# Attention heads sent in pairs, and the values of the sink heads held stationary

## The chip, the cores and the metric

The kernel runs on one core of a Trainium2 chip. The metric is the device time of one execution in microseconds (us): the median of three runs is 1763.69 us, the lowest 1762.58 and the highest 1768.16. Below, TensorE is the matrix engine (PE in the rows, its weight loads PEld), VectorE is DVE, ScalarE is ACT, and SP is the engine that issues the loads.

## The reference, cut to what matters

Two model blocks follow each other; everything is float32, 256 tokens of width 1024. The first block (three recurrent branches and a feed-forward) is not touched. The second block runs two layers over the stream `x` and, in the first layer only, over 256 tokens of context `ctx`. In each layer the normed tokens are projected, and the mixing has three parts whose outputs, 256 + 512 + 256 columns wide, go through `w_out`:

```
a  gated MLP over chunks of 128 tokens
b  8 query heads of 64, 2 key heads: softmax(q k^T / 8 with a sink logit) v
     p = softmax([window scores, context scores, sink]);  o = p_window v + p_ctx v_ctx
c  4 differential heads: softmax(q1 k1^T) - lam softmax(q2 k2^T), times v, then a norm
```

Queries of `x` see 512 keys (256 of the stream, of which a window mask leaves |q - k| <= 128, and 256 of the context). Queries of the context see the 256 context keys. The sink is one more logit per head: it enters the sum of the softmax, and has no value.

## The kernel before

Products are done in float32 precision by splitting each operand into a high and a low part and summing three products (high x high, high x low, low x high); this holds for all projections (`gemm_ws`, `gemm_xs`, `mm3`) and for the scores. Every weight comes from memory as a tile of up to 512 KB (`weight_raw`), is cast to its high part by ScalarE (L383) and its low part is taken by VectorE (L385). The products of the probabilities with the values are plain float32, which the trace shows as two instructions each.

`layer` (from L1364) handles one layer of the second block. Queries, keys and values of 128 tokens are a tile; `t` 0 and 1 are the stream, 2 and 3 the context. `unit` projects, `qk_part` norms and rotates queries and keys and transposes them into `qkh` and `qkl` (heads on partitions: two heads of 64, or four maps of 32, per column of blocks). `HEADORDER` puts heads j and j + 4, which belong to different key heads, side by side, so that a pair lies on rows 0 to 63 and 64 to 127.

`attention` (from L1609) sends a list of items through a pipeline of steps, a `yield` after each. A query tile has 12 items: 8 window heads and 4 differential heads. In a step, `scores` is emitted for an item two ahead, `transposed` for one, `values` for the one before, and `finished` for one still older:

- `scores` calls `probs` once for a window head and twice for a differential head. `probs` takes a bank of the pool `c`, sends three products (L1517 to L1519, 64 or 32 rows, 128 columns stationary, 512 or 256 streaming) and for the tiles 0 and 1 of a window head adds the mask as a product with an identity over 256 columns (L1521). VectorE takes the maximum (L1523) and makes the bias from it (L1525, L1527); ScalarE takes the exponential and its sum (L1529).
- `transposed` turns the probabilities over in blocks of 128 on TensorE (L1562) into one bank of the pool `s`; ScalarE copies them to SBUF (L1564).
- `values` multiplies: the transposed probabilities are stationary, the 128 columns of the values stream (L1574). For a window head the product holds both key heads, and half of it is used. After four heads VectorE divides by the sum with the sink, straight from the bank of the pool `o` into `OB` (L1585).
- `finished` transposes `OB` (L1606) and splits it into `XH` and `XL`, from which `out_proj` multiplies by `w_out`.

Tiles 3 and 2 of layer 0 run between the projections of the stream, four steps after each unit; tiles 1 and 0 of layer 0 run with the output projection of the context, a weight after the steps in `Knobs.fill`; in layer 1 only tiles 1 and 0 run, with steps of the modulation after the steps in `Knobs.afill`. PSUM has eight banks, shared out by `psum`: two for projections (`g`), three for scores (`c`), one for outputs (`o`) and two for transposes (`s`); in the attention of layer 1, four for scores, one for outputs, two for transposes and one for the modulation (`a`).

The program is written in the order above, but each engine's final order is made by the framework's scheduler when it is built: in the trace, pieces of neighbouring steps and projections stand between each other. Within the built program every engine works in its given order; TensorE's records, though, show products on different rows starting side by side.

Of the kernel before, what the change touches and what calls it, by code (L numbers as in the profile page):

```python
# [10 lines left out]
F32 = mybir.dt.float32  # L11
# [17 lines left out]
# columns of the modulations done on the tensor engine, 512 at a time, and on the vector engine, 128  # L29
# [4 lines left out]
# column offsets of the first block's w_in  # L34
# [4 lines left out]
# rows of the small projections: i gates, f gates, dt  # L39
# [3 lines left out]
def _ws(name, layer, c0, nk=8, r0=0):  # L43
    """[nk*128, 128] block of a weight, rows on partitions, 128 columns."""
    def cut(w):
        return w[name][layer][r0:r0 + nk * 128, c0:c0 + 128].reshape(nk, 128, 128).transpose(1, 0, 2)
# [12 lines left out]
def _ada(layer, c0, q):  # L59
    """[256, 512] block: rows on partitions, 512 columns."""  # L60
# [27 lines left out]
def _qcols(c):  # L88
    """256 columns of the window attention's queries, heads j and j + 4 side by side."""
    return np.concatenate([np.arange(512 + 64 * h, 576 + 64 * h) for h in HEADORDER[4 * c:4 * c + 4]])  # L90

# [33 lines left out]
def plan2(layer):  # L125
# [10 lines left out]
    p += [(("out", j), _ws("w_out_2", layer, 128 * j)) for j in range(8)]  # L136
# [12 lines left out]
def _cols(v):  # L149
    """[n*128] -> [128, n]"""  # L150
# [3 lines left out]
def _convc(w):  # L154
    """[K, n*128] -> [128, n*K]"""
# [121 lines left out]
class Knobs:  # L277
# [11 lines left out]
    fill = (2, 6, 10, 14, 18, 22, 24, 26)  # L289
    afill = tuple(range(20, 30))  # L290
# [9 lines left out]
def tile_two_blocks(ctx: ExitStack, tc: tile.TileContext, xT, ctxT, cst1, cst, cstw, pb1, pl0, pl1, pf0, pf1, pc, pcb, wb, w0, w1, out,  # L300
# [16 lines left out]
    class PS:  # L317
        """PSUM pools of the phase at hand"""

    def psum(**bufs):  # L320
        """Shares out the eight banks: name=number."""
# [3 lines left out]
        for nm in "asgcpo":  # L325
            if nm not in bufs:
                setattr(PS, nm, None)

# [64 lines left out]
    def gained(dst_h, dst_l, x, g):  # L393
        """x g, split: what the first products after a norm take; 1 / rms is applied to their results"""
# [4 lines left out]
    def mm3(o, w, rhs, nk, late=False, first=True, last=True):  # L399
        """o = W^T x in three passes; late: the low part of x comes last."""  # L400
# [19 lines left out]
    def gemm_xs(ph, keys, lhs, toks, evac):  # L420
        """out[128 tokens, 256 features]; lhs(k, t) gives (high, low) of a token tile."""
        w = [weight(ph, k, 256) for k in keys]
        for t in toks:
            ps = PS.g.tile([128, 512], F32, tag="g", name="psx")
# [11 lines left out]
    def rsqrt_raw(pool, a, n, tag, bufs, rows=128):  # L436
        """RS * result = 1 / sqrt(a)"""
# [3 lines left out]
        # in two halves, so that neither waits for the step before  # L441
# [13 lines left out]
    def mean_sq(x, scale=None, eps=EPS):  # L455
        """mean of squares + eps, [128 tokens, 2 blocks of them], in PSUM"""
# [20 lines left out]
    def rms_all(a):  # L477
        """[128, 256] on every partition: 1 / (RS sqrt(a)) for tokens on partitions"""
# [44 lines left out]
    def ada_pe(li):  # L523
        """512 columns at a time on the tensor engine; both parts of the conditions share a pass."""
# [35 lines left out]
    def ada_rows(pool):  # L560
        """twice silu(c) of both conditions, on every partition"""
# [9 lines left out]
    def ada_dve(li):  # L571
        """128 columns at a time, on partitions: products summed along the rows"""
# [11 lines left out]
    def ada_tick():  # L584
        """After each weight tile: now and then a step."""
# [16 lines left out]
    # =====================================================================  # L602
    # convolution, SwiGLU, down projection
    # =====================================================================
    def ffn(ph, pool, halves, xh, xl, cw3, cb, causal, resid, hook=None, mid=None, raw=None):
        """halves: 1 or 2 blocks of 256 tokens. With two, the first columns take the second block first and the
        last rows the first block first, so that neither waits for the other's norms."""
# [20 lines left out]
        def down(j0, j1, m, rhs, n):  # L628
            ps = PS.g.tile([128, 512], F32, tag="g", name="psg")
# [7 lines left out]
        for j0, j1 in CHUNKS:  # L637
            hid = []
            for j in range(j0, j1):
# [3 lines left out]
                elif j == 0:  # L643
                    # as many as there are buffers take the second block first
                    w = [weight(ph, ("up", e // 2, e % 2), 128) for e in range(3)]
                    first = [PS.g.tile([128, 512], F32, tag="g", name="psg") for _ in range(3)]
# [36 lines left out]
    # =====================================================================  # L683
    # first block
# [1084 lines left out]
```

## Time and profile before

| What | Value |
|---|---|
| median of 3 runs | 1763.69 us |
| lowest, highest | 1762.58, 1768.16 us |
| profiled execution, first to last instruction | 1767.7 us |
| TensorE busy | 1738.8 us, 98% |
| VectorE busy | 1384.8 us, 78% |
| ScalarE busy | 983.7 us, 56% |
| mean granted TensorE clock | 0.991 of full |
| the 16 DMA engines, main queue | 49.8% of their span |

The profile is of one execution, and its own time is known as its span, 1767.7 us, which lies among the three runs, near the highest. Busy times of TensorE include the modelled end of each product, so products that stream behind each other overlap in it: the start of one row to the start of the next is what a product keeps the engine for. A timeline row merges equal instructions that follow each other: start, length, engine, line, operation, output and inputs, shape (rows*columns of the stationary part, then what streams), count, and in brackets the idle time before it.

### The profile page before, as it was taken

How to read it: one execution, taken by the hardware profiler on the slowest of the kernel's cores; microseconds unless marked ns; L12 is line 12 of the kernel's file. 1: busy time of each engine (PE TensorE's matmuls, PEld its weight loads, DVE VectorE, ACT ScalarE, POOL GpSimd, SP SyncE). 2: the span in 40 equal slices, each digit the busy share in tenths (PEclk: the TensorE clock that was granted, in tenths of full speed). 3: DMA queues.
4: the chain of work that ended last, by engine and by line, in shares of the span. 5: the costliest groups of instructions: out<-in, count | busy, mean ns of one | idle time of the engine just before them, and what ended most of it. 6: DMA issues, size and time to landing. Idle time of an engine off the chain costs nothing.

```text
span 1767.7 us, 31912 instructions
## 1 busy us (share of the span) xinstructions
PE 1738.8 (98%) x12442; PEld 1568.2 (89%) x12442; DVE 1384.8 (78%) x2716; ACT 983.7 (56%) x1723; POOL 0.2 (0%) x4
## 2 busy tenths in 40 slices
PE   7999999999999999999999999999999999999999
PEld 7999988878888999999878898888888997799999
DVE  7987967557778996877687799999656878788776
ACT  6655645445556865666676564442244556766554
POOL 0000000000000000000000000000000000000000
PEclk8999999999999999999989999999999999999999
DMA  7555445447677666654211356657433543046564
GB/s 233 159 154 152 138 132 157 147 126 222 218 228 228 187 190 221 209 170 139 86 67 47 105 163 189 183 171 232 129 96 107 168 132 120 24 141 195 174 196 132
DMA packets 80502, 276.97 MB, mean 157 GB/s; under 512 B 9056, under 2 KB 13792, under 8 KB 80224
## 3 DMA queue, kind: packets, MB, share of 16 engines
q1 hardware_dynamic: 80352, 274.94, 49.8%
q8 instruction: 98, 1.61, 0.4%
q14 instruction: 52, 0.43, 0.1%
HBM read 273.86 MB, written 1.05 MB: 156 GB/s over the span
## 4 chain that ended last, share of the span: by engine, by line
PE 51%; DVE 3%; ACT 1%; issue 0%; ACTq 0%
PE psg L404 12%; PE psg L407 12%; PE psg L406 11%; PE pso L1574 3%; PE psx L429 2%; PE psx L431 2%; PE psx L430 2%; PE psp L1562 2%; PE psc L1517 1%; PE psc L1519 1%; PE psc L1518 1%; DVE wl L385 0%; ACT Pp L1529 0%; DVE mx L1523 0%; PE psc L1521 0%
## 5 line engine op out<-in xcount | busy, mean ns | idle before, releaser
L383 ACT CAST wh<-raw 128x1024 fp32r<-128x1024 f32 (+1 forms) x475 | 490.9, 1037 | 531.0 <-PE psg L406 423.7
L385 DVE TENSOR_TENSOR wl<-raw,wh 128x1024 fp32r<-128x1024 f32 (+1 forms) x475 | 572.5, 1208 | 206.8 <-ACT wh L383 203.2
L404 PE MATMUL psg<-XH,wh 128*128 128x256 f32 (+1 forms) x1288 | 400.7, 314 | 3.6 <-ACT XH L390 1.9
L407 PE MATMUL psg<-XH,wl 128*128 128x256 f32 (+1 forms) x1288 | 398.8, 312 | 0.3 <-DVE wl L385 0.3
L406 PE MATMUL psg<-XL,wh 128*128 128x256 f32 (+1 forms) x1240 | 387.5, 313 | 0.7 <-DVE XL L1304 0.5
L404 PEld LDWEIGHTS psg<-XH,wh 128*128 128x128 f32 x1288 | 243.0, 189 | 22.0 <-ACT XH L390 2.3
L407 PEld LDWEIGHTS psg<-XH,wl 128*128 128x128 f32 x1288 | 243.3, 189 | 15.9 <-DVE wl L385 1.0
L406 PEld LDWEIGHTS psg<-XL,wh 128*128 128x128 f32 x1240 | 234.5, 189 | 16.1 <-DVE XL L1304 1.1
L404 PE MATMUL psg<-xh,wh 128*128 128x256 f32 x704 | 203.4, 289 | 1.8 <-ACT xh L390 1.3
L406 PE MATMUL psg<-xl,wh 128*128 128x256 f32 x704 | 200.5, 285 | 0.9 <-DVE xl L391 0.9
L407 PE MATMUL psg<-xh,wl 128*128 128x256 f32 x704 | 200.1, 284 | 0.3 <-DVE wl L385 0.3
L404 PE MATMUL psg<-hh,wh 128*128 128x256 f32 (+1 forms) x592 | 179.6, 305 | 0.1
L407 PE MATMUL psg<-hh,wl 128*128 128x256 f32 (+1 forms) x592 | 178.5, 302 | 0.0
L406 PE MATMUL psg<-hl,wh 128*128 128x256 f32 (+1 forms) x592 | 178.5, 302 | 0.0
L404 PEld LDWEIGHTS psg<-xh,wh 128*128 128x128 f32 x704 | 134.9, 192 | 6.0 <-ACT xh L390 1.5
L406 PEld LDWEIGHTS psg<-xl,wh 128*128 128x128 f32 x704 | 135.1, 192 | 2.9 <-DVE xl L391 1.4
L407 PEld LDWEIGHTS psg<-xh,wl 128*128 128x128 f32 x704 | 134.9, 192 | 2.2 <-issue 1.3
L406 PEld LDWEIGHTS psg<-hl,wh 128*128 128x128 f32 x592 | 111.5, 188 | 5.3 <-DVE hl L391 0.2
L404 PEld LDWEIGHTS psg<-hh,wh 128*128 128x128 f32 x592 | 110.9, 188 | 5.9 <-ACT hh L390 0.6
L407 PEld LDWEIGHTS psg<-hh,wl 128*128 128x128 f32 x592 | 111.2, 188 | 5.5
L429 PE MATMUL psx<-wh,XH 128*128 128x256 f32 x384 | 110.0, 287 | 1.1 <-DVE ss L1379 0.5
L430 PE MATMUL psx<-wh,XL 128*128 128x256 f32 x384 | 108.5, 283 | 0.0
(435 smaller groups left out, 3237.8 us busy)
## 6 DMA issues: line engine op xcount, KB each, us to landing
raw<-w SPq DMA_DIRECT2D x254, 512.0 KB, 3.7
raw<-wb SPq DMA_DIRECT2D x197, 512.0 KB, 4.3
araw<-w SPq DMA_DIRECT2D x40, 512.0 KB, 4.2
raw<-w SPq DMA_DIRECT2D x16, 384.0 KB, 3.4
raw<-wb SPq DMA_DIRECT2D x8, 384.0 KB, 3.2
xres<-xT SPq DMA_DIRECT2D x16, 128.0 KB, 3.6
plt<-pl SPq DMA_DIRECT2D x2, 588.0 KB, 5.5
xres<-ctxT SPq DMA_DIRECT2D x8, 128.0 KB, 2.7
```

The lines of the kernel that those rows point to most:

```text
L383: S.copy(wh[:, 0:sz], raw[:, 0:sz])
L385: V.tensor_tensor(wl[:, 0:sz], raw[:, 0:sz], wh[:, 0:sz], ALU.subtract)
L404: T.matmul(o, wh[:, k], xh, start=(first and k == 0), stop=False)
L406: T.matmul(o, wh[:, k], xl, start=False, stop=False)
L407: T.matmul(o, wl[:, k], xh, start=False, stop=(last and not late and k == nk - 1))
L429: T.matmul(o, xh, wh[:, k % 4], start=(k == 0), stop=False)
L430: T.matmul(o, xl, wh[:, k % 4], start=False, stop=False)
L431: T.matmul(o, xh, wl[:, k % 4], start=False, stop=(k == 7))
L1517: T.matmul(o, qh, kh, start=True, stop=False)
L1518: T.matmul(o, qh, kl, start=False, stop=False)
L1562: T.transpose(ps[:, b], p[:, b * 128:(b + 1) * 128], ident)
L1574: T.matmul(po[:, i % 4], pt[:, b], v, start=(b == 0), stop=(b == nb - 1))
```

## The change

The items of a query tile become 8: four pairs of window heads and four differential heads. `scores` sends the two tiles of an item alternately: high x high of both, then high x low of both, then low x high of both. The mask is a product over the 128 columns in which there is anything masked, once for each tile of a pair. `transposed` takes up to four blocks per bank: a pair with 512 keys fills two banks, the first copied by ScalarE, the second by VectorE. For window heads, `values` holds 64 columns of the values stationary and streams the transposed probabilities, so that the output comes with features on partitions, the two heads of a pair in the halves. The division by the sum is therefore along the free dimension: the reciprocal is broadcast over 64 partitions by a product with the identity into a bank of `s`, copied by ScalarE, and multiplied in by VectorE; the result is split into `XH` and `XL` without a transpose. `OB` and `finished` are for the differential heads alone. The order of the features changes with it, and so do the rows of `w_out` (`_mixrows`, done when the weights are laid out).

The banks of the first and second stage become `c` 4, `o` 1, `s` 3, and projections take theirs from `s` (`PS.gtag`); in the attention of layer 1 the shares stay. `fill` and `afill` follow the shorter list of steps. All other differences are comments. Its core:

```diff
-    fill = (2, 6, 10, 14, 18, 22, 24, 26)
-    afill = tuple(range(20, 30))
+    fill = (1, 3, 6, 8, 11, 13, 15, 17)
+    afill = tuple(range(10, 20))
...
+        PS.gtag = "g"
+        if PS.g is None:
+            PS.g, PS.gtag = PS.s, "s"
...
-        ps = PS.g.tile([128, 512], F32, tag="g", name="psg")
+        ps = PS.g.tile([128, 512], F32, tag=PS.gtag, name="psg")
...
-        psum(g=2, c=3, o=1, s=2)
+        psum(c=4, o=1, s=3)
...
         def scores(A, i):
...
+            rows = []
+            for e in range(2):
+                if i < 4:
+                    d = slice(64 * e, 64 * e + 64)
+                    rows.append((d, i, 4, 2 * i + e, L.nsink[:, 2 * i + e:2 * i + e + 1]))
+                else:
+                    m = 2 * i - 8 + e
+                    d = slice(32 * (m % 4), 32 * (m % 4) + 32)
+                    rows.append((d, 5 + m // 4, 7 + m // 4, 10 + m, None))
+            ps = [PS.c.tile([128, 512], F32, tag="c", name="psc") for _ in range(2)]
+            kk = slice(A.k0, A.k0 + A.nk)
+            mask = i < 4 and A.t < 2
+            for q_, k_, n in ((qkh, qkh, 0), (qkh, qkl, 1), (qkl, qkh, 2)):
+                for e, (d, jq, jk, h, _) in enumerate(rows):
+                    T.matmul(ps[e][:, 0:A.nk], q_[d, jq, A.tq], k_[d, jk, kk], start=(n == 0),
+                             stop=(n == 2 and not mask))
+            if mask:
+                o = slice(128 * (1 - A.t), 128 * (1 - A.t) + 128)
+                for e in range(2):
+                    T.matmul(ps[e][:, o], identb, winb[:, A.t, o], start=False, stop=True)
...
+        def transposed(A, pp):
+            out = []
+            blocks = [(p, b) for p in pp for b in range(A.nb)]
+            for i in range(0, len(blocks), 4):
+                some = blocks[i:i + 4]
+                ps = PS.s.tile([128, 4, 128], F32, tag="s", name="psp")
+                for n, (p, b) in enumerate(some):
+                    T.transpose(ps[:, n], p[:, b * 128:(b + 1) * 128], ident)
+                pt = ap.tile([128, 4, 128], F32, tag="PT", name="PT", bufs=Knobs.ptb)
+                if i:
+                    V.tensor_copy(pt[:, 0:len(some)], ps[:, 0:len(some)])
+                else:
+                    S.copy(pt[:, 0:len(some)], ps[:, 0:len(some)])
+                out += [pt[:, n] for n in range(len(some))]
+            return [out[j:j + A.nb] for j in range(0, len(out), A.nb)]
...
         def values(A, i, pt):
...
+            if i < 4:
+                for b in range(nb):
+                    for e in range(2):
+                        d = slice(64 * e, 64 * e + 64)
+                        T.matmul(po[d, i], BV[:, kb0 + b, d], pt[e][b], start=(b == 0), stop=(b == nb - 1))
+            else:
+                for b in range(nb):
+                    T.matmul(po[:, i - 4], pt[0][b], CV[:, kb0 + b, (i - 4) // 2 * 128:(i - 4) // 2 * 128 + 128],
+                             start=(b == 0), stop=(b == nb - 1))
+            if i == 3:
+                es = tiny.tile([128, 8], F32, tag="es", name="es")
+                V.tensor_tensor(es, A.nm, P("sink"), ALU.add)
                 S.activation(out=es, in_=es, func=AF.Exp)
+                V.tensor_tensor(es, es, A.sums, ALU.add)
                 V.reciprocal(es, es)
+                ps = PS.s.tile([128, 4, 128], F32, tag="s", name="psrs")
+                for j in range(4):
+                    for e in range(2):
+                        T.matmul(ps[64 * e:64 * e + 64, j], es[:, 2 * j + e:2 * j + e + 1].to_broadcast([128, 64]),
+                                 ident, start=True, stop=True)
+                rs = ap.tile([128, 512], F32, tag="scr", name="rsb", bufs=Knobs.scr)
+                S.copy(rs, ps.rearrange("p j q -> p (j q)"))
+                V.tensor_tensor(rs, rs, po.rearrange("p j q -> p (j q)"), ALU.mult)
+                r4 = rs.rearrange("p (j q) -> p j q", j=4)
+                split(XH[:, 2:6, A.tm], XL[:, 2:6, A.tm], r4)
...
+        def finished(A):
             ps = PS.s.tile([128, 4, 128], F32, tag="s", name="pso2")
+            for j in range(2):
+                T.transpose(ps[:, j], A.OB[:, j * 128:(j + 1) * 128], ident)
+            split(XH[:, 6:8, A.tm], XL[:, 6:8, A.tm], ps[:, 0:2])
...
-                items += [(A, i) for i in range(12)]
+                items += [(A, i) for i in range(8)]
```

## Rows read from the trace of the kernel before

**Rows 1.** The page, busy time by engine (share of the span), instructions.

```profile
PE 1738.8 (98%) x12442; PEld 1568.2 (89%) x12442; DVE 1384.8 (78%) x2716; ACT 983.7 (56%) x1723; POOL 0.2 (0%) x4
```

**Rows 2.** Windows: stretch, length; busy us (count) PE, PEld, DVE, ACT, POOL; clock; DMA.

```profile
828.00:920.50 92.50, 90.99 (x639) 79.73 (x640) 67.06 (x211) 64.85 (x152) 0.00 (x0) 0.94 0.29 92
920.50:1003.00 82.50, 81.98 (x570) 67.29 (x570) 63.33 (x204) 53.77 (x117) 0.00 (x0) 0.98 0.15 46
...
1479.60:1552.00 72.40, 71.33 (x475) 53.05 (x475) 51.09 (x149) 48.49 (x106) 0.00 (x0) 1.00 0.19 58
```

**Rows 3.** Timeline, TensorE, layer 1: start us, length us, line, tiles, count.

```profile
1510.07 0.50 PE L1517 MATMUL psc<-qkh 64*128 64x512 f32 x1
...
1510.96 0.28 PE L1521 MATMUL psc<-winb,identb 128*128 128x256 bf16 x1
1511.08 0.60 PE L1562 MATMUL psp<-ct,Pp 128*128 128x128 f32 x4
1511.52 1.06 PE L1574 MATMUL pso<-CV,PT 128*128 128x128 f32 x8
1512.50 0.50 PE L1517 MATMUL psc<-qkh 64*128 64x512 f32 x1
```

**Rows 4.** Timeline, TensorE, layer 1, a differential item.

```profile
1499.33 0.51 PE L1517 MATMUL psc<-qkh 32*128 32x512 f32 x2
...
1500.22 0.66 PE L1562 MATMUL psp<-ct,Pp 128*128 128x128 f32 x4
```

**Rows 5.** Timeline, TensorE, layer 0, a head of a short tile.

```profile
845.08 0.38 PE L1517 MATMUL psc<-qkh 64*128 64x256 f32 x1
...
845.63 0.44 PE L1562 MATMUL psp<-ct,Pp 128*128 128x128 f32 x2
845.90 0.61 PE L1574 MATMUL pso<-BV,PT 128*128 128x128 f32 x4
846.44 0.38 PE L1517 MATMUL psc<-qkh 64*128 64x256 f32 x1
```

**Rows 6.** Timeline, TensorE, layer 0, products of the gated MLP.

```profile
826.88 1.09 PE L1497 MATMUL psmix<-plt,AV 128*64 128x128 f32 x16
827.90 0.38 PE L1517 MATMUL psc<-qkh 64*128 64x256 f32 x1
```

**Rows 7.** Timeline, TensorE, layer 1, transposes of the output.

```profile
1509.54 0.60 PE L1606 MATMUL pso<-ct,OB 128*128 128x128 f32 x4
```

**Rows 8.** Timeline, TensorE, layer 0, a differential item.

```profile
987.30 0.49 PE L1517 MATMUL psc<-qkh 32*128 32x512 f32 x1
...
988.87 0.66 PE L1562 MATMUL psp<-ct,Pp 128*128 128x128 f32 x4
```

**Rows 9.** Groups by line, 1479.6 to 1552: busy us, mean ns, idle before.

```profile
L1523 DVE TENSOR_REDUCE mx<-psc 128x1 f32<-128x512 f32 x32 | 21.8, 684 | 8.5 <-PE psc L1521 6.0 <-PE psc L1519 2.2
...
L1556 DVE SCALAR_TENSOR_TENSOR Pp<-Pp,cf 128x512 f32<-128x512 f32 x8 | 6.0, 747 | 0.1
L1527 DVE SCALAR_TENSOR_TENSOR nm<-mx,NS,nsink 128x1 f32<-128x1 f32 x16 | 3.3, 213 | 0.3
...
L1585 DVE TENSOR_TENSOR OB<-pso,es 128x128 f32<-128x128 f32 x8 | 1.9, 284 | 3.5 <-PE pso L1574 3.5
...
L1529 ACT ACTIVATE Pp<-psc,nm,ss 128x512 f32<-128x512 f32 x32 | 24.8, 777 | 4.6 <-DVE nm L1525 2.7 <-DVE nm L1527 1.5
L1564 ACT COPY PT<-psp 128x512 f32<-128x512 f32 x24 | 14.0, 585 | 11.8 <-PE psp L1562 11.8
L1529 ACT ACTIVATION_READ_ACCUMULATOR Pp<-psc,nm,ss 128x1 f32 x32 | 6.2, 195 | 0.0
```

**Rows 10.** Windows of 6 us in layer 0, columns as in rows 2.

```profile
906.00:912.00 6.00, 4.87 (x22) 4.26 (x21) 6.00 (x19) 4.88 (x13) 0.00 (x0) 0.50 0.15 33
...
936.00:942.00 6.00, 6.00 (x55) 5.84 (x53) 6.00 (x16) 4.87 (x12) 0.00 (x0) 1.00 0.10 12
```

**Rows 11.** Tile psx: what its engines, idle, waited for (us, times).

```profile
  ACT QK L1391: 0.6, 2
```

More of the change, by code (lines that the diff above doesn't have):

```diff
@@ L90, in _qcols, with _mixrows @@
     return np.concatenate([np.arange(512 + 64 * h, 576 + 64 * h) for h in HEADORDER[4 * c:4 * c + 4]])
+def _mixrows():
+    heads = [np.arange(256 + 64 * h, 320 + 64 * h) for h in HEADORDER]
+    return np.concatenate([np.arange(256), *heads, np.arange(768, 1024)])
 def _ffn_plan(up, down, layer):
@@ L135, in plan2 @@
     p += [(("au", j), _ws("w_in_2", layer, 128 * j)) for j in range(2)]
-    p += [(("out", j), _ws("w_out_2", layer, 128 * j)) for j in range(8)]
+    p += [(("out", j), _ws("w_out_2", layer, 128 * j, rows=_mixrows())) for j in range(8)]
     p += _ffn_plan("w_up_2", "w_down_2", layer)
@@ L317, in tile_two_blocks @@
     class PS:
+        pass
     def psum(**bufs):
@@ L423, in gemm_xs @@
         for t in toks:
-            ps = PS.g.tile([128, 512], F32, tag="g", name="psx")
+            ps = PS.g.tile([128, 512], F32, tag=PS.gtag, name="psx")
             o = ps[:, 0:256]
@@ L645, in ffn @@
                     w = [weight(ph, ("up", e // 2, e % 2), 128) for e in range(3)]
-                    first = [PS.g.tile([128, 512], F32, tag="g", name="psg") for _ in range(3)]
+                    first = [PS.g.tile([128, 512], F32, tag=PS.gtag, name="psg") for _ in range(3)]
                     for c in reversed(H):
@@ L1547, in scores @@
-            pp = []
-            for i in (2 * i - 16, 2 * i - 15):
-                d = slice(32 * (i % 4), 32 * (i % 4) + 32)
-                pp.append(probs(A, (d, 5 + i // 4), (d, 7 + i // 4), False, 10 + i, None,
-                                sums[:, i:i + 1], nm[:, i:i + 1]))
-            i, rc = i - 1, A.rc
-            V.reciprocal(rc[:, i:i + 2], sums[:, i:i + 2])
+                A.rc = tiny.tile([128, 8], F32, tag="rc", name="rc")
+                A.dsums = tiny.tile([128, 8], F32, tag="dsums", name="dsums")
@@ new lines, in scores @@
+            sums, nmt = (A.sums, A.nm) if i < 4 else (A.dsums, A.dnm)
+            pp = []
+            for e, (d, jq, jk, h, nsink) in enumerate(rows):
+                c = h if i < 4 else h - 10
+                o, nm = ps[e][:, 0:A.nk], nmt[:, c:c + 1]
+                mx = tiny.tile([128, 1], F32, tag="mx", name="mx")
+                V.tensor_reduce(mx, o, AX.X, ALU.max)
+                if nsink is None:
+                    V.tensor_tensor(nm, mx, NS[:, A.t, h:h + 1], ALU.mult)
+                else:
+                    V.scalar_tensor_tensor(nm, mx, NS[:, A.t, h:h + 1], nsink, ALU.mult, ALU.min)
+                p = ap.tile([128, 512], F32, tag="P", name="Pp", bufs=Knobs.pb)
+                S.activation(out=p[:, 0:A.nk], in_=o, func=AF.Exp, scale=ss[:, A.t, h:h + 1], bias=nm,
+                             accum_out=sums[:, c:c + 1])
+                pp.append(p)
@@ L1559, in transposed @@
-        def transposed(A, p):
-            ps = PS.s.tile([128, 4, 128], F32, tag="s", name="psp")
-            for b in range(A.nb):
-                T.transpose(ps[:, b], p[:, b * 128:(b + 1) * 128], ident)
-            pt = ap.tile([128, 4, 128], F32, tag="PT", name="PT", bufs=Knobs.ptb)
-            S.copy(pt[:, 0:A.nb], ps[:, 0:A.nb])
-            return pt
-        def values(A, i, pt, sums, nm):
+            return pp[:1]
+        def transposed(A, pp):
[13 more added lines that the diff above has]
+            return [out[j:j + A.nb] for j in range(0, len(out), A.nb)]
@@ L1568, in values @@
+        def values(A, i, pt):
             kb0, nb, OB = A.k0 // 128, A.nb, A.OB
-            if i % 4 == 0:
+            if i in (0, 4):
                 A.po = PS.o.tile([128, 4, 128], F32, tag="o", name="pso")
             po = A.po
-            for b in range(nb):
-                v = BV[:, kb0 + b] if i < 8 else CV[:, kb0 + b, (i - 8) // 2 * 128:(i - 8) // 2 * 128 + 128]
-                T.matmul(po[:, i % 4], pt[:, b], v, start=(b == 0), stop=(b == nb - 1))
-            if i in (3, 7):
-                h4 = slice(i - 3, i + 1)
-                es = tiny.tile([128, 4], F32, tag="es", name="es")
-                V.tensor_tensor(es, nm[:, h4], P("sink")[:, h4], ALU.add)
+            if i < 4:
+                for b in range(nb):
+                    for e in range(2):
+                        d = slice(64 * e, 64 * e + 64)
+                        T.matmul(po[d, i], BV[:, kb0 + b, d], pt[e][b], start=(b == 0), stop=(b == nb - 1))
+            else:
+                for b in range(nb):
[4 more added lines that the diff above has]
+                V.tensor_tensor(es, A.nm, P("sink"), ALU.add)
@@ L1580, in values @@
                 S.activation(out=es, in_=es, func=AF.Exp)
-                V.tensor_tensor(es, es, sums[:, h4], ALU.add)
+                V.tensor_tensor(es, es, A.sums, ALU.add)
                 V.reciprocal(es, es)
-                for s_ in range(2):
-                    c = (4 * s_ + (i - 3) // 2) * 64
-                    V.tensor_tensor(OB[:, c:c + 128].rearrange("p (h d) -> p h d", d=64),
-                                    po[:, s_::2, 64 * s_:64 * s_ + 64],
-                                    es[:, s_::2].unsqueeze(2).to_broadcast([128, 2, 64]), ALU.mult)
```

69 lines of the change are left out of this document (18 added, 51 removed).

## Prediction

> **What bounds the kernel now.** I read the busy shares first, then the timeline of TensorE in the attention, then busy time by stage, and last the VectorE and ScalarE groups of one such stage. The shares [rows 1] show TensorE busy for 98% of the span. Its ends are modelled, so I trust the starts: from one row's start to the next kind's start is what a piece costs. Attention runs in three stages [rows 2]: the context's tiles 3 and 2 in layer 0 (828 to 920 us, mixed with projections), tiles 1 and 0 in layer 0 (920.5 to 1003), the same tiles in layer 1 (1479.6 to 1552). In all three TensorE is busy nearly throughout, VectorE for 67 of 92, 63 of 82 and 51 of 72 us, ScalarE a little less than VectorE. So TensorE's work sets these stages, with VectorE 5 to 30% behind it. Four query tiles are long (512 keys), two are short (256 keys).
>
> **Scores in pairs.** A window head uses 64 of the 128 rows and goes alone. For a long tile its three products and the mask take from 1510.07 to 1511.08, 1.01 us [rows 3], so two heads 2.02. What two tiles on different rows cost is already in the trace: the differential maps, on 32 rows each, start in twos (x2 in the first row) and their six products take 0.89 us until the transposes begin [rows 4]. That is one map's time, so they run side by side. A window pair after the change should do so too: 0.89 plus two masks of 128 columns, together the 0.12 of one mask of 256 (1510.96 to 1511.08), makes 1.01. Saved 1.01 per pair; 4 long tiles of 4 pairs make 16: 16.2 us. In a short tile a head takes 0.55 (845.08 to 845.63) [rows 5]; the pair the same instead of 1.10: 0.55 x 8 = 4.4 us.
>
> **Values stationary.** For a long tile a head's eight instructions (four products, two each) take 0.98 us [rows 3], two heads 1.96. After the change there are 16 instructions with 64 columns stationary and 128 streaming, the two heads in different halves of the columns. The gated MLP's products have that very shape, and 16 of them take from 826.88 to 827.90, 1.02 us with entry and exit [rows 6]. Saved 0.94 x 16 = 15.0 us. In a short tile a pair costs 1.08 (845.90 to 846.44, twice) [rows 5] and should cost about half of 1.02, or 0.55 with the fixed part: 0.53 x 8 = 4.2 us. The transposes stay: eight a pair at 0.44 per four [rows 3].
>
> The Trainium skill, "TensorE: Matmul & The Clock Gate", Part 3 (The mechanism), says that a weight load overlaps running matmuls only when its row group differs. Heads in different column halves share all row groups, so by that rule this part's loads would stand bare, and the saving on values would go. The 16 products of the MLP in 1.02 us [rows 6] speak against it: they share the rows too.
>
> **The sink's scale.** It was applied by VectorE to the output; now it is broadcast by eight products (16 instructions, 1.02 us by the same row), in exchange for the four output transposes, 0.53 us (1509.54 to 1510.07) [rows 3, 7]. Plus 0.49 x 6 tiles = 2.9 us.
>
> **Fourth score bank in layer 0.** There, with three, the second map's products often come after the first's (x1): from 987.30 to the transposes at 988.87, 1.57 us [rows 8] against 0.89. I find four such items of eight in the second stage, worth up to 2.9 us; the item may be held by VectorE instead, so between 0 and 2.9 I take 1.5.
>
> **Sum on TensorE:** 16.2 + 4.4 + 15.0 + 4.2 - 2.9 + 1.5 = 38.4 us.
>
> **The new wait.** The broadcast products need the sums of all eight heads, their exponential on ScalarE and a reciprocal on VectorE; before, only VectorE needed these. On ScalarE this small exponential stands behind the next item's two exponentials, 2 x (0.777 + 0.195), and a copy of 0.585; on VectorE behind two maxima, 2 x (0.684 + 0.213) [rows 9]. From the end of the next item's scores: 0.9 to the first exponential, 1.94 for two, 0.6 for the copy, 0.7 for the four small steps: 4.1 us. TensorE has eight transposes and the values, 1.9 us, to do meanwhile; behind the broadcast in its queue stand the next scores, and for them wait VectorE's maxima. So at most 2.2 us a tile; nothing, if other products are put ahead. The output bank also stays occupied one copy (0.585) and one product on VectorE (about 0.68) longer, with scores and transposes, about 1.4 us, as cover. I take 1.2 us x 6 = 7.2; the ends are 0 and 13.
>
> **VectorE.** It takes over half of the transposes' copies for long tiles: four a tile, priced like the maximum of the same 128x512 in PSUM, 0.684 [rows 9] (a bare copy may be 0.1 less, and ScalarE's takes 0.585). Plus 2.7, plus 0.7 for the scaling, minus four scalings of 0.284, minus three small steps of 0.16: plus 1.8 a tile, 3.6 per stage of two. In the second stage that makes 63.3 + 3.6 = 66.9 us, against TensorE's 82.0 - 8 x 1.95 + 1.0 - 1.5 + 2.4 = 68.3: two engines at their limit in one stretch, neither of which can be. I add 2 us there. In layer 1 it is 54.7 against 59.1, in the first stage about 70 against 84; nothing added. ScalarE loses these copies (2.3 a tile) and gains one.
>
> **Fill.** The eight output projections and the modulation steps are spread over 20 steps instead of 28, one to two steps apart, with the same products; moved, not added. Their DMAs keep their order on SP's queue, and the DMA share of those stages is 0.15 to 0.29 [rows 2], so I cost that at nothing; without that cover a weight of 512 KB would be late by some us once or twice.
>
> **Result.** 38.4 - 7.2 - 2 = 29.2 us off the profiled execution's span of 1767.7. That execution is 4.0 above the median of the runs, 1763.69; 1763.7 - 29.2 = 1734.5, so 1735. With all open terms at their ends (TensorE's full 38.4 + 1.4, no wait; or 13 us of waits and 8 for VectorE) it is 1724 to 1747: the forecast's own range.
>
> **Rivals.**
> (1) VectorE takes over as the bound. For it: it is within 2 us of TensorE in the second stage, it is full in whole 6 us slices there already (936 to 942, 6.00 of 6 [rows 10]), and differential items cost it two maxima and a product of 0.747 [rows 9]. Against it: stages one and three have slack. If only half of each stage's saving comes through, about 15 us: 1749. The Trainium skill, "TensorEngine Tiling (Array Packing)", PSUM Bottleneck, says that tiling speeds up TensorE but not the emptying of PSUM, which would then be next; that is this rival.
> (2) The change does half of what it says: scores or values do not run side by side, because the scheduler puts other products between, or loads don't overlap. The twos [rows 4] and the 16 products in 1.02 us [rows 6] speak against it. Without the values' 19.2 us the saving is 10: 1754.
> (3) The clock falls. From 906 to 912, after TensorE had begun to idle, the granted clock was 0.50 (1.2 GHz) and 22 matmuls went through, against 55 at 1.00 in 936 to 942 [rows 10]. If gaps behind VectorE bring this to 45 us of attention, streaming takes twice as long and waits take what they took; I take 1.6 times: plus 27, which eats the gain: about 1762. Against it: at 1498 to 1510, where TensorE waits a little in each item, the products still go at full speed [rows 4].
> (4) Slower: the projections lose their own two PSUM banks and share three with the transposes. They take 62 bank tiles in the two layers (40 and 22 by the code), each of which may now wait for an older transposes' copy. Before, such waits were 0.6 us in all [rows 11]. Break-even is 29 / 62 = 0.47 us a tile; at 0.7 it is plus 43 - 29 = 14: 1778. Against it: a bank is held for some 3 us at most, and three are turned over in the time of one projection tile.
>
> **Chances.** Forecast 0.60, VectorE 0.17, half 0.08, clock 0.08, shared banks 0.07. Less than 0.3% (5.3 us) a measurement of this kernel can hardly tell from no change. The first three cases lie beyond it: faster 0.85. Clock splits: same 0.06, and with the banks slower 0.09. The range: 1722 to 1757 holds the forecast with its ends, VectorE and half.
>
> **What would show it.** Window items' scores start in twos and take 0.9 to 1.0 us per pair; value products come 16 in about 1.0 us; the stages shrink to about 85, 70 and 60 us; the idle time before the broadcast products is 1 to 2 us a tile. Wrong it is if these products come singly, if the maxima are always ready before VectorE gets to them while TensorE idles, if the granted clock in the attention falls below 0.9, or if projections idle behind the transposes' copies.

## The result

The changed kernel takes 1781.99 us (median of 4 runs, 1780.56 to 1785.72), the kernel before 1765.93 on the same chip. The ratio is 1.0083, 95% interval 1.0058 to 1.0108: slower by 15 us, where 29 us less was forecast.

The page of the changed kernel first, busy time by engine:

```profile
span 1778.2 us, 32002 instructions
...
PE 1713.4 (96%) x12514; PEld 1543.8 (87%) x12514; DVE 1388.2 (78%) x2696; ACT 967.9 (54%) x1693; POOL 0.2 (0%) x4
```

TensorE works 25 us less than in [rows 1], yet the span is 10.5 us longer: it idles more. The timeline of layer 1 shows what its pieces cost (they answer to [rows 3, 4, 6]):

```profile
1513.89 1.09 PE L1603 MATMUL pso<-PT,BV 128*64 128x128 f32 x16
1514.91 0.51 PE L1545 MATMUL psc<-qkh 32*128 32x512 f32 x2
...
1516.40 1.09 PE L1603 MATMUL pso<-PT,BV 128*64 128x128 f32 x16
1517.33 1.04 PE L1617 MATMUL psrs<-ct,es 128*64 128x128 f32 x16
1518.30 0.50 PE L1545 MATMUL psc<-qkh 32*128 32x512 f32 x2
...
1521.19 1.16 PE L1606 MATMUL pso<-CV,PT 128*128 128x128 f32 x8 [0.68 <-DVE rsb L1621]
...
1531.34 0.50 PE L1545 MATMUL psc<-qkh 64*128 64x512 f32 x2
...
1532.24 0.28 PE L1551 MATMUL psc<-winb,identb 128*128 128x128 bf16 x2
1532.36 1.05 PE L1584 MATMUL psp<-ct,Pp 128*128 128x128 f32 x8
```

From start to start: a window pair's scores and masks 1.02 us (1531.34 to 1532.36), its values 1.02 (1513.89 to 1514.91), the sink's broadcast 0.97. These are the sizes of the forecast. So the time was lost elsewhere. Two windows of 6 us ahead of the context's attention show where (columns as in [rows 2]):

```profile
812.00:818.00 6.00, 1.47 (x13) 1.23 (x11) 5.81 (x21) 3.16 (x6) 0.00 (x0) 1.00 0.62 174
818.00:824.00 6.00, 4.54 (x20) 4.03 (x21) 5.81 (x24) 2.09 (x5) 0.00 (x0) 0.51 0.21 79
```

TensorE is nearly idle while VectorE norms and rotates the context's queries and keys; then the clock is at 0.51. The timeline of TensorE around the final norm's sums shows another such place:

```profile
768.34 0.36 PE L475 MATMUL psn<-onesn,sq 128*128 128x1 f32 x2
771.80 0.59 PE L475 MATMUL psn<-onesn,sacc 128*128 128x1 f32 x2 [3.10 <-DVE sacc L483]
...
775.39 1.19 PE L492 MATMUL psr<-ct,rcy 128*128 128x128 f32 x4 [1.72 <-DVE rcy L461]
777.04 0.58 PE L439 MATMUL psx<-wh,XH 128*128 128x256 f32 x1 [0.46 <-ACT rr L494]
...
812.87 0.60 PE L1477 MATMUL pst<-ct,QK 128*128 128x128 f32 x4
819.12 2.15 PE L1477 MATMUL pst<-ct,QK 128*128 128x128 f32 x9 [5.66 <-DVE QK L1462]
821.61 1.33 PE L1477 MATMUL pst<-ct,QK 128*128 128x128 f32 x5 [0.34 <-DVE qkl L401]
822.68 0.58 PE L414 MATMUL psg<-XH,wh 128*128 128x256 f32 x1
```

The sums' products (L475) and the broadcast of the norm (L492) stand alone from 766.35 to 777.04, and so do the transposes of queries and keys (L1477) from 812.87 to 822.68. In the kernel before, projections (psx) run between the sums:

```profile
769.74 0.38 PE L465 MATMUL psn<-onesn,sacc 128*128 128x1 f32 x2
770.49 0.36 PE L429 MATMUL psx<-wh,XH 128*128 128x256 f32 x1 [0.37 <-DVE xres L1316]
...
771.28 0.28 PE L429 MATMUL psx<-wh,XH 128*128 128x256 f32 x1
771.40 0.28 PE L465 MATMUL psn<-onesn,sq 128*128 128x1 f32 x2
```

Of stage A, from the first of these sums to the first score, TensorE is idle for 0.6 us before and for 12.4 us after, and the granted clock (column after the engines) is lower; before, then after:

```profile
769.70:827.90 58.20, 57.59 (x488) 56.58 (x486) 43.91 (x106) 37.45 (x70) 0.00 (x0) 1.00 0.46 146
```

```profile
766.40:842.00 75.60, 63.20 (x489) 61.62 (x488) 44.27 (x106) 37.80 (x70) 0.00 (x0) 0.89 0.37 112
```

By stages, with the same landmarks in every kernel: A runs from the first of those sums to the first score, B to the first mask product of the stream's tiles, C to the last output transpose of layer 0, P from the first projection of layer 1 to its first score, D to its last output transpose. Profiled executions, us; what comes ahead of A varied between 762.9 and 771.8 among all kernels here, so the last line counts from A to the end. Names are those of the experiments below.

| | before | after | own banks | before, shared | other place | own banks, copies on ScalarE |
|---|---|---|---|---|---|---|
| A | 58.2 | 75.6 | 58.4 | 75.8 | 66.3 | 58.2 |
| B | 90.4 | 93.3 | 94.4 | 90.1 | 92.2 | 94.4 |
| C | 89.4 | 83.8 | 80.1 | 95.9 | 84.3 | 77.2 |
| P | 72.9 | 77.5 | 73.2 | 79.3 | 77.6 | 72.9 |
| D | 73.5 | 68.6 | 70.7 | 73.0 | 65.9 | 67.2 |
| A to end | 997.9 | 1011.8 | 989.6 | 1028.2 | 1004.2 | 984.0 |

The change lost 17.4 us in A, where no attention runs, 2.9 in B and 4.6 in P, and gained 5.6 in C and 4.9 in D. P is projections too.

Each column is one execution, and a stage can differ by about 3 us for a reason other than the edit. In D the changed kernel and *other place* run the same instructions in the same order on TensorE, VectorE and ScalarE, and their first 6.6 us are alike. Then the granted clock is at 0.50 in the one and at 1.00 in the other, so that 28 products pass against 56, and D is 2.7 us longer. The changed kernel first, then *other place*:

```profile
1494.10:1500.70 6.60, 5.02 (x28) 2.28 (x27) 6.47 (x12) 4.59 (x9) 0.00 (x0) 1.00 0.50 152
1500.70:1507.50 6.80, 6.80 (x28) 4.51 (x27) 3.16 (x7) 4.61 (x11) 0.00 (x0) 0.50 0.41 152
```

```profile
1490.10:1496.70 6.60, 5.02 (x28) 2.25 (x27) 6.40 (x12) 4.60 (x9) 0.00 (x0) 1.00 0.60 164
1496.70:1503.50 6.80, 6.80 (x56) 4.63 (x55) 5.60 (x12) 6.37 (x15) 0.00 (x0) 1.00 0.40 146
```

### The profile page after: what moved, and what is told of

The parts are those of the page before. It is cut to its first block, busy times and chain, and to the rows that moved or that the text cites. A ratio compares the mean times of both kernels' runs of the same rounds, so it can differ in the third digit from the quotient of the medians.

```text
span 1778.2 us, 32002 instructions
## 1 busy us (share of the span) xinstructions
PE 1713.4 (96%) x12514; PEld 1543.8 (87%) x12514; DVE 1388.2 (78%) x2696; ACT 967.9 (54%) x1693; POOL 0.2 (0%) x4
## 4 chain that ended last, share of the span: by engine, by line
PE 85%; DVE 9%; ACT 3%; issue 1%; DMA 1%; SPq 0%; DVEq 0%; ACTq 0%
PE psg L414 21%; PE psg L417 20%; PE psg L416 20%; PE psx L439 3%; PE psx L441 3%; PE psx L440 3%; DVE wl L395 2%; PE psc L1545 2%; PE psl L878 1%; PE psada L551 1%; PE psada L552 1%; ACT wh L393 1%; PE psp L1584 1%; DVE mx L1558 1%; PE pso L1606 1%
## 5 line engine op out<-in xcount | busy, mean ns | idle before, releaser
L441 PE MATMUL psx<-wl,XH 128*128 128x256 f32 x384 | 110.0, 286 | 0.0
```

The costliest lines, as they stand in the source:

```text
L441: T.matmul(o, xh, wl[:, k % 4], start=False, stop=(k == 7))
```

## The experiments

Ratios are to the kernel before, with 95% intervals from five rounds. My theory was rival 4: projections now share three banks with the transposes and lie where the sums were. Against it stood that the attention itself had become slower.

**Own banks** (the changed kernel, banks as before).

```diff
-        psum(c=4, o=1, s=3)
+        psum(g=2, c=3, o=1, s=2)
```

> The changed kernel with the banks of before in the first stages of both layers (two for projections, three for scores, one for outputs, two for transposes). Theory S (the shared banks cost the time): the stretch from the first projection of layer 0 to the first score goes back from 64.9 to about 57 us, the sum of squares before it no longer holds TensorE for 9 us, layer 1's projections go from 77 back to about 73; the pairs then stand alone, less some waits for a third score bank: 1750 us (1742 to 1758). Theory I (the pairs themselves, or the order that the scheduler makes of the shorter list of items, cost it): the time stays near 1782 (1776 to 1786).

Measured: 1756.9 us, 0.9938 (0.9924 to 0.9951). One line turns the loss into a gain; the new shares cost the changed kernel 1.45% of 1766, 25.6 us.

**Before, shared** (the kernel before, with the changed kernel's shares; its projections take their banks from `s`, as the changed kernel's do).

```diff
...
-        psum(g=2, c=3, o=1, s=2)
+        psum(c=4, o=1, s=3)
```

> The kernel before with the shares of after in the first stages: four score banks, one for outputs, three that transposes and projections share. Theory S: it loses what the changed kernel lost outside the attention, about 20 us, and gains up to 3 from the fourth score bank: 1784 us (1778 to 1790). Theory I: no loss, 1763 to 1767.

Measured: 1795.78 us, 1.0157 (1.0137 to 1.0177): 27.7 us by the new shares alone, above the range expected. A loses 17.6 us and P 6.4, as in the changed kernel; C loses 6.5 too, where a fourth score bank was to gain up to 3. So the loss is the banks', with or without pairs.

**Other place** (the changed kernel, the shared banks placed first).

```diff
-        psum(c=4, o=1, s=3)
+        psum(s=3, c=4, o=1)
```

> The changed kernel with the three shared banks placed first (where the feed-forward's projections lay) and not last (where the norm's sums lay). Theory S in the form that the place is what costs at the start (new projections wait until the sums of squares leave the same banks): the first 6 to 7 us come back, the rest does not: 1775 us (1772 to 1778). Theory S in the form that only the sharing itself costs: 1782. Theory I: 1782.

Measured: 1774.97 us, 1.0042 (1.0028 to 1.0055). A regains 9.3 of its 17.4 us, P nothing. About half of A's loss is the place: shares are taken over the banks of the phase before, and the first projections waited for the sums that stood there. The rest is then the sharing, which the next run bears out.

**Staged** (shared while there is no attention, own banks from there).

```diff
-        psum(c=4, o=1, s=3)
+        psum(g=4, s=4)
...
+            psum(g=2, c=3, o=1, s=2)
```

> The changed kernel with four banks for projections and four for transposes until the attention of a layer begins, then in layer 0 the shares of before (two, three, one, two). Theory S: at least as good as the own banks of before, since no scores are under way in that time: 1747 us (1738 to 1756). Theory I: about 1780.

Measured: 1766.67 us, 0.9991 (0.9981 to 1.0002). That is above the range expected. A is 67.2, since these pools lay over the sums' banks again; P falls to 69.3, below before. Here nothing is shared in A, so the place alone costs 9.0 us (67.2 for 58.2); *other place* has the sharing alone, 8.1 us (66.3 for 58.2). Together they are 17.1 of the 17.4 us that the change lost in A.

**Staged, off the sums** (`g=3, s=5` in layer 0, `g=4, s=4` in layer 1; in layer 0 own banks from the context's attention, and four score banks with one for projections from the stream's).

```diff
-        psum(c=4, o=1, s=3)
+        psum(g=4, s=4) if last else psum(g=3, s=5)
...
+            psum(g=2, c=3, o=1, s=2)
...
+            psum(g=1, c=4, o=1, s=2)
```

> Pairs with banks by stage: until the attention three banks for projections and five for transposes in layer 0 (so that the projections' lie where the feed-forward's projections lay, not on the norm's sums), four and four in layer 1; then two, three scores, one output, two transposes in layer 0; for the stream's attention in layer 0 one for projections, four scores, one, two. Theory P+S (e4 lost its time at the start because its new banks lay on those of the sums, and pairs want four score banks): the start is as in e1 (58 us from the sums to the first score), the stream's attention in layer 0 falls from 80 to 77 us, layer 1 stays at 142: 1752 us (1747 to 1756). If the place is not the cause of e4's loss, it starts as late as e4: 1762 or more.

Measured: 1757.73 us, 0.9948 (0.9936 to 0.996). A is back at 58.2, P stays at 69.0. As a whole it does not differ from own banks.

**Copies on ScalarE** (own banks; the second copy of a pair's transposes goes to ScalarE).

```diff
-                if i:
+                if False:
```

> As e1_own_banks, but all copies of transposed probabilities on ScalarE, as before the change; VectorE has 2.7 us less per long tile, ScalarE 2.4 us more. Theory V (VectorE sets the attention stages now that TensorE needs less): faster by up to 4 stages' tiles x 2.7, say 5 to 10 us: 1749 us (1745 to 1753). Rival (TensorE, or the chain through both, sets them): 1757, or slower by up to 5 if ScalarE's queue then holds the exponentials back.

Measured: 1752.07 us, 0.9914 (0.9902 to 0.9927), the lowest ratio of all; its interval and that of own banks (from 0.9924) just touch. C falls by 2.9 and D by 3.5 us, as theory V has it: VectorE has 8 copies of a 128x512 tile less in each of these stages. How much of D's 3.5 us is VectorE's is not shown, as the clock stood at 0.50 there for 3.4 us, with own banks for 10.2.

**Banks and copies** (the last two together).

> The banks by stage of e8_staged_banks and all copies on ScalarE as in e7_copies_act, four steps a unit as in both. If the two add up (e8 took 5 us off e1 in the trace, e7 6, both in the stream's attention and layer 1): 1748 us (1744 to 1753). If each gave back the same wait: 1752, as e7 alone.

Measured: 1755.8 us, 0.9947 (0.9928 to 0.9966). They don't add up: P gains 3.6 us, B, C and D are 0.8, 2.2 and 4.9 longer than with the copies alone. Against the same banks without the copies (staged, off the sums), C and D are 1.9 and 2.4 longer and the ratio is the same, 0.9947 for 0.9948. So the gain by the copies is shown with own banks alone.

**One by one** (own banks; the tiles of a pair are sent one after the other).

```diff
-            for q_, k_, n in ((qkh, qkh, 0), (qkh, qkl, 1), (qkl, qkh, 2)):
-                for e, (d, jq, jk, h, _) in enumerate(rows):
+            for e, (d, jq, jk, h, _) in enumerate(rows):
+                for q_, k_, n in ((qkh, qkh, 0), (qkh, qkl, 1), (qkl, qkh, 2)):
...
-                for b in range(nb):
-                    for e in range(2):
+                for e in range(2):
+                    for b in range(nb):
```

> As e1_own_banks, but the two heads of a pair are sent one after the other, in the scores and in the values, and not alternately. Theory Q (TensorE takes products on other rows or columns ahead of their turn, as the differential maps of before show, which stood one after the other in the built program): the same time, 1755 to 1759, and pairs still within 0.01 us of each other. Rival (only alternate sending lets them run side by side): values cost 1.96 us a pair again and scores 2.0, plus 20 us: 1775 or more.

Measured: 1763.84 us, 0.9986 (0.9973 to 1.0), 7 us more than own banks, between the two forecasts. Its timeline:

```profile
1491.84 1.58 PE L1603 MATMUL pso<-PT,BV 128*64 128x128 f32 x16
1493.35 0.50 PE L1545 MATMUL psc<-qkh 32*128 32x512 f32 x2
...
1494.24 0.66 PE L1584 MATMUL psp<-ct,Pp 128*128 128x128 f32 x4
```

The scores still start in twos, though the program, as built too, has three of one map and then three of the other; the values take 1.51 us (1491.84 to 1493.35) instead of 1.02. Sending alternately is worth 0.49 us a pair for the values, nothing for the scores.

**Why does B not shrink?** With own banks TensorE idles there, and VectorE is full (windows as in [rows 10]):

```profile
906.00:912.00 6.00, 3.23 (x23) 2.37 (x21) 6.00 (x20) 2.70 (x5) 0.00 (x0) 0.96 0.00 1
912.00:918.00 6.00, 4.82 (x16) 2.71 (x17) 4.70 (x13) 1.17 (x3) 0.00 (x0) 0.50 0.12 18
```

VectorE norms and rotates the stream's last queries there. The context's attention, now shorter, ends before them at four steps a unit, so three runs spread it: three steps a unit (with own banks; with banks and copies), and two (with banks and copies).

```diff
-    ra = 4
+    ra = 3
```

> Pairs with the banks of before (as e1_own_banks), and the context's attention spread over the projections three steps a unit, not four, so that its 23 steps again reach into the norms of the stream's queries, as the 31 of before did. Theory F (in e1 the context's attention ends too early, and TensorE has nothing to do beside the norms and rotations, 903 to 918 us, where the granted clock fell to 0.5 for 10 us): the stretch from the first score to the first mask of layer 0 falls from 94 to about 87 us: 1750 us (1746 to 1754). Rival D (this stretch is set by VectorE's chain of norms and rotations however TensorE is filled): 1757, as e1.

> As e9_all_ra2 with three steps a unit. Between: sums to mask 148 us, 1747 us (1741 to 1752); the rival says 1750, as for two steps.

> The pairs with the banks by stage of e8_staged_banks, all copies of transposed probabilities on ScalarE as in e7_copies_act, and the context's attention spread two steps a unit. If the three findings add up (banks by stage 5 us against e1, copies 6, and the stream's queries projected some 15 us earlier, so that their norms and rotations no longer stand bare): from the sums to the first mask 145 us (e1 152.8, before 148.6), the stream's attention in layer 0 75, layer 1 137: 1744 us (1738 to 1750). Rival (that stretch is a chain on VectorE and filling it only moves the wait): sums to mask 150 or more, 1750.

Measured: 1759.63 us, 0.996 (0.9946 to 0.9974); 1754.02, 0.9938 (0.992 to 0.9955); 1763.55, 0.9979 (0.9968 to 0.9991). The two with three steps are no better than their parents: with own banks B falls to 85.5, but A rises to 64.1 and C to 84.3. A and B together fall by 3.2 us, C rises by 4.2: A to C is 232.9 with four steps, 233.9 with three. The wait moves. Two steps cost about 6 us (0.9979 for 0.9947).

**Less rotation** (own banks and copies; the sine part of the rotation is left out, so the output is not the reference's).

> As e7_copies_act, but of the rotation only the product with the cosines is done; the products with the sines and their sum are left out. VectorE has some 4 us less per token tile of the stream, 8 us a layer, all of it between the stream's projections and its first scores; TensorE's and ScalarE's work is the same. Theory V (once TensorE needs less, VectorE's chain of norms and rotations sets the stretch ahead of the stream's scores): sums to first mask 153 falls to 145 to 148, layer 1 140 to 134 to 137: 1742 us (1737 to 1746). Rival (TensorE's order or its clock sets these stretches): 1750 to 1753, as e7.

Measured: 1753.47 us, 0.9926 (0.991 to 0.9943), no change. B falls by 7.3 us, C rises by 6.9: after 916 TensorE has no projections left beside the first steps of the stream's attention, and the clock is at 0.50 for 13.7 us from 921.7.

**Less difference** (own banks and copies; in differential heads the second map is subtracted over 8 columns alone, so that part of the output is not the reference's), and the same edit of the kernel before.

```diff
-            V.scalar_tensor_tensor(pp[0][:, 0:A.nk], pp[1][:, 0:A.nk], cf, pp[0][:, 0:A.nk], ALU.mult, ALU.add)
+            V.scalar_tensor_tensor(pp[0][:, 0:8], pp[1][:, 0:8], cf, pp[0][:, 0:8], ALU.mult, ALU.add)
```

> The kernel with own banks and all copies on ScalarE, in which the second map of a differential head is subtracted over 8 of its columns alone (so the differential part of the output is not the reference's). VectorE loses about 0.65 us for each of 8 differential items of a stage of long tiles: 5.2 us in the second stage and 5.2 us in layer 1 (0.747 us a subtraction before); all waits stay where they are. Theory V (VectorE paces the differential items once TensorE's window items are shorter): layer 1's attention 67.2 to about 63 us, second stage 77.2 to about 73, median 1752 to about 1744. Rival H (what is left over is at the head and the tail of each pipeline, where TensorE waits for the chain of one item, whatever VectorE's load): stages within 1.5 us of 67.2 and 77.2, median 1750 to 1753.

> The kernel before with the same edit: the second map of a differential head is subtracted over 8 columns alone (the differential part of the output is not the reference's). VectorE loses the same 5.2 us in each long stage. Theory V: TensorE sets these stages before the change, so the second stage stays at 89.4 and layer 1 at 73.5 within 1.5 us, median 1763 to 1766. If instead the differential items were paced by VectorE already before, both stages lose 3 to 4 us and the median is about 1758.

Measured: 1752.08 us, 0.9923 (0.9906 to 0.9941), and 1764.91, 0.9991 (0.9979 to 1.0002). The medians don't move, as rival H has it; the stages split the theories. D goes from 67.2 to 63.8 with the clock at 0.50 for 3.4 us in both, in the kernel before only from 73.5 to 73.4; C stays (77.2 and 77.2, before 89.4 and 88.8). So in these executions VectorE paces layer 1 after the change and did not before; the second stage it does not. The reading rests on one execution of each kernel, and the profiled one with less difference is the fastest of its six (1745.28 us); 3.4 us are 0.19%, less than the width of either interval. TensorE's timeline shows a pair where VectorE holds it up, first with copies on ScalarE, then with less difference:

```profile
1492.46 0.49 PE L1545 MATMUL psc<-qkh 64*128 64x512 f32 x1
1492.80 0.39 PE L1545 MATMUL psc<-qkl,qkh 64*128 64x512 f32 x1
1492.92 0.49 PE L1545 MATMUL psc<-qkh 64*128 64x512 f32 x1
1493.03 0.39 PE L1545 MATMUL psc<-qkh,qkl 64*128 64x512 f32 x1
1493.26 0.39 PE L1545 MATMUL psc<-qkl,qkh 64*128 64x512 f32 x1
1493.49 0.39 PE L1545 MATMUL psc<-qkh,qkl 64*128 64x512 f32 x1
1493.81 0.28 PE L1551 MATMUL psc<-winb,identb 128*128 128x128 bf16 x2
```

```profile
1492.76 0.50 PE L1545 MATMUL psc<-qkh 64*128 64x512 f32 x2
1493.10 0.40 PE L1545 MATMUL psc<-qkl,qkh 64*128 64x512 f32 x2
1493.33 0.40 PE L1545 MATMUL psc<-qkh,qkl 64*128 64x512 f32 x2
1493.66 0.28 PE L1551 MATMUL psc<-winb,identb 128*128 128x128 bf16 x2
```

The second bank of this pair comes late: its products trail the first's, and the scores take 1.35 us until the mask instead of 0.90. That VectorE's maxima free it late is argued from the edit.

## Why the prediction was wrong

The sign was wrong because of rival 4, which had 0.07, and the size was wrong beside it: with its own banks the change gains 11 us (0.62%), not 29. For the three stages some 7.5, 12.5 and 12.4 us less were forecast (92.5, 82.5 and 72.4 to about 85, 70 and 60); with own banks, by landmarks a little different, B is 4.0 us longer, C 9.3 and D 2.8 shorter.

**The step that failed** is the argument against rival 4: "a bank is held for some 3 us at most, and three are turned over in the time of one projection tile", with waits of 0.6 us in [rows 11] as its base. So the sum had no term for the new shares, and they cost 25.6 us. That row tells what an arrangement with own banks waits for, not what sharing would. The same view of the changed kernel (tile `psx`, here from 760 to 1000 us: what its engines, idle, waited for; us, times) doesn't show the loss even now:

```profile
  PE psx L441: 23.8, 14
  ACT rr L494: 1.2, 2
```

The first line is ScalarE waiting for projections; TensorE waits 1.2 us ahead of them, because the built order has them behind the transposes and the sums, whose tiles show the wait. A pool's tiles are taken in turn: a projection that comes behind a transpose gets its bank after it, and the transpose itself waits for VectorE, 5.66 us at 819. The runs show the cost and its places; that the turn is what orders them so is argued. Spread over my 62 tiles, 25.6 us are 0.41 a tile, near the break-even of 0.47. But the waits come as two blocks and not tile by tile, and part of A's is the place of the shares over the sums, which the prediction did not look at: no row of the attention shows it, the `psum` calls do.

**Scores in pairs, values, sink's scale:** right. 1.02 for 1.01, 1.02 for 1.02, 0.97 for 1.02 us. These are the costs of the products alone, without waits. The Trainium skill, "TensorE: Matmul & The Clock Gate", Part 3 (The mechanism), says that loads overlap running products only when the row group differs, which would have left the values' loads bare; the same section also lets a load into the background weight buffer run ahead. The 16 products in 1.02 us, whose 16 loads lie between 1513.89 and 1514.74, overlap them, as the second allows and the first does not.

**The new wait:** 1.2 us a tile was forecast before the broadcast. In this row it lies a step later: the next values wait 0.68 us for the output bank (1521.19, behind `rsb`), and the broadcast follows the values at once.

**VectorE:** "In layer 1 it is 54.7 against 59.1", with nothing added, was wrong as far as the one execution with less difference shows. With own banks layer 1 (D) gains 2.8 us; the copies on ScalarE give 3.5 more (in part perhaps the clock's), less difference another 3.4. I compared sums over a stage, where items differ. A reading was off as well: [rows 2] put VectorE 23 to 28% behind TensorE, not 5 to 30. VectorE's groups in layer 1, with copies on ScalarE (columns as in [rows 9]):

```profile
L1558 DVE TENSOR_REDUCE mx<-psc 128x1 f32<-128x512 f32 x32 | 21.1, 685 | 6.5 <-PE psc L1551 4.4 <-PE psc L1545 2.1
...
L1573 DVE SCALAR_TENSOR_TENSOR Pp<-Pp,cf 128x512 f32<-128x512 f32 x8 | 6.0, 751 | 0.2
L1562 DVE SCALAR_TENSOR_TENSOR nm<-mx,NS,nsink 128x1 f32<-128x1 f32 x16 | 2.9, 214 | 0.0
L1560 DVE TENSOR_TENSOR dnm<-mx,NS 128x1 f32<-128x1 f32 x16 | 2.2, 155 | 0.0
L1572 DVE SCALAR_TENSOR_TENSOR cf<-rc,nlam,dsums 128x1 f32<-128x1 f32 x8 | 1.7, 218 | 0.2
...
L1570 DVE RECIPROCAL rc<-dsums 128x2 f32<-128x2 f32 x8 | 1.3, 163 | 3.9 <-ACT Pp L1564 3.8
```

A differential item takes 2 x (0.685 + 0.155) + 0.163 + 0.218 + 0.751 = 2.81 us of VectorE, and of TensorE 0.89 + 0.44 + 0.98 = 2.31 [rows 3, 4]: it was VectorE's before, too. But two window heads took TensorE 2 x (1.01 + 0.44 + 0.98) = 4.86 us [rows 3] and VectorE 2 x (0.685 + 0.214) = 1.80, so VectorE caught up there; now a pair takes TensorE about 3.0. The Trainium skill, "TensorEngine Tiling (Array Packing)", PSUM Bottleneck, says that after a fourfold speedup of TensorE the emptying of PSUM may come next and should be shared by ScalarE and VectorE. That VectorE comes next fits layer 1; giving all of these copies to ScalarE was a little better here than sharing them with own banks (0.9914 against 0.9938), and no better with banks by stage (0.9947 against 0.9948).

**Head of the pipeline:** not in the sum at all. In layer 1 the first values come 8.75 us after the first score before the change, 12.14 with own banks and copies on ScalarE (12.04 with less difference). The four score banks are filled in 2.1 us instead of 4.2, and then TensorE waits for the same exponentials:

```profile
1469.21 0.50 PE L1545 MATMUL psc<-qkh 64*128 64x512 f32 x1 [2.22 <-ACT Pp L1564]
...
1471.37 1.70 PE L1584 MATMUL psp<-ct,Pp 128*128 128x128 f32 x7
1473.00 0.79 PE L1545 MATMUL psc<-qkh 64*128 64x512 f32 x2
```

After that gap seven transposes take 1.63 us, at half the clock. The clock is part of the head's length: in the changed kernel it is 13.88 us, in *other place*, the same order at full clock, 10.86. The head's 3.4 us and VectorE's 3.4 would together cover the 6.1 that layer 1, 6.3 us better with copies on ScalarE, still lacks of its 12.4; that the head's 3.4 reach the end of D is not shown.

**The first stage:** "about 85" was wrong; B is 94.4 with own banks, 90.4 before. With own banks TensorE spends 34.0 us there on scores, transposes, values, the sink's broadcast and the output's transposes (from start to next start), 40.6 before: the gain is there. But 52 more products of the context's output projection were drawn in (124 products into `psg` for 72, some 0.12 us each, 6 us), and the wait for VectorE's rotation came out behind them. The clock's fall (rival 3) goes with these gaps: 0.50 for 56 us of the changed kernel's span, 31 before, 20 with own banks and copies on ScalarE. It makes the waits dearer, and the same waits don't always bring it: D has 6.8 us of it in the changed kernel and none in *other place*.

**Still open:** why gains in single stages of layer 0 don't reach the end. Spreading the steps and less rotation moved 4 to 9 us from one of A, B, C to another. Head of the second stage and the rotation seem to wait for each other's filler, but no run isolates that.

## What to carry to other kernels

Price a change of PSUM shares as a change of its own: run the new shares on the old kernel, and look at which banks of the phase before the new pools lie on. Where an engine's work is cut in half, compare the engines item by item and at the head of the pipeline, not by stage sums alone. Before a stage's 3 us are put down to an edit, compare the granted clock in it. And the filler that hid a chain before may have been the work that you removed.

## What the runs showed of the hardware

Products on different rows, written three and three, start in twos in the record and take 0.90 us, like those written alternately. Products in different column halves, written eight and eight, take 1.51 us against 1.02 alternately: about half the overlap is lost, as if TensorE took only a few of the coming products ahead of their turn. No run varied that number. The granted clock stood at 0.50, 1.2 GHz, for 10.2 us from 770.3 in the changed kernel, behind the lone sums, and for 6.8 us from 818.1, behind a window with 1.47 us busy of 6; the products behind such a gap take up to twice as long, so it is paid for again. It does not fall after every such gap: after 6.6 us with the same 28 products and 5.02 us busy, it fell in layer 1's attention of the changed kernel and not in that of *other place*, at a price of 2.7 us.
